# Conv accumulators, z gate, SSD outputs and the scaled x in PSUM instead of SBUF

## The chip, the core and the metric

One core of one Trainium2 chip. The metric is the device time of one execution in microseconds (us); the median of three runs of the kernel before is 935.29 us.

## The reference, cut to what matters

One decoder layer, on a prompt of 1024 tokens and on 8 samples of 8 tokens, with a width of 1024, all in float32:

- h = RMSNorm(x); one projection gives z (1024 columns), xBC (1536), dt, pool inputs and gates.
- xBC goes through a causal depthwise convolution of width 4 (four taps per channel plus a bias) and SiLU. It gives x (16 heads of 64), B and C (2 groups of 128 states).
- SSD in chunks of 128 tokens, per head: y = (mask(C Bt) * decay) (x*dt) + exp(acum) * (C h), and the state h is multiplied by the chunk's decay and gets Bt (x*dt*decay_to_end) added.
- y + d_skip * x, times SiLU(z), then a grouped RMSNorm; a pooling branch beside it; two branch maps with sigmoid gates, an output projection, a norm and the residual.

## The kernel before

Activations lie with channels on the 128 partitions and tokens along the free dimension: 1088 columns (1024 prompt tokens, 64 sample tokens) in three chunks of 256, 384 and 448. A product with a weight matrix takes three float32r passes (hi*hi, lo*hi, hi*lo), so one group of a slab of 128 output channels and one chunk is 24 matmuls of 128x256, 128x384 or 128x448 into one PSUM bank.

The order of the work is written out by slots. `main[t]` is one such group of matmuls. `at_pe(t, f)` puts f's TensorE work ahead of it, `at(t, f, key)` puts work of the other engines behind it, sorted by key. Each engine runs its instructions in that order. So in slot t the other engines work on what the slots before have left, while TensorE runs `main[t]`.

The stages that the change touches:

- **Conv** (slots 0 to 36, twelve slabs). Group t gives three steps: `evac` in slot t+1 (ScalarE copies the bank to R in SBUF and writes A = R * tap 0 + bias; GpSimd fills the three halo columns of R), `taps` in slot t+2 (three VectorE operations A = R shifted * tap + A, key 5: the last of the slot), `fin` in slot t+3 (ScalarE tanh, VectorE (T+1)*A into the tile of x, B or C, key 1).
- **SSD units** (`Unit`: chunk c, four heads u). Units of the first state group run one to a slot in slots 22 to 37, beside conv. Those of the second group run two to a slot in slots 40 to 48, beside the z gates. For a unit at slot t: `xT` in slot t-2 (TensorE transposes x into a bank `xb`, for every second unit B and C too), `prep` (VectorE: x0 = x*dt), `xprod` (GpSimd: x1 = x0*decay_to_end), and in slot t-1 `xsplit` (ScalarE copies x1 to hi, VectorE subtracts to lo); in slot t `mats` (TensorE, into a bank `pyo` for y and a bank `pst` for the state), `fade` (GpSimd), `out` (VectorE: two operations on E, two on x) and `state` (VectorE). `bc_post` splits B and masks C Bt out of the same `xb` bank.
- **Z gates** (`ZTile.gate`, slots 38 to 61): ScalarE tanh, VectorE (T+1)*z into T, VectorE x*0.5*T.

Scratch tiles of 512 columns come from `rt`, a pool of six SBUF buffers that rotates. PSUM has eight banks: two each of `m0` (the groups), `pyo`, `xb` and `pst`.

Of the kernel before, what the change touches and what calls it, by code (L numbers as in the profile page):

```python
# [13 lines left out]
ALU = mybir.AluOpType  # L14
# [23 lines left out]
def hybrid_decoder_step(  # L38
# [258 lines left out]
    class Conv:  # L297
# [14 lines left out]
        def group(self, c):  # L312
            t, box = group3(self.slab, c, hrhs)
            at(t + 1, self.evac, c, box, key=0)
            at(t + 2, self.taps, c, key=5)
            at(t + 3, self.fin, c, key=1)
            return t

        def evac(self, c, box):
            a, b = CHUNKS[c]  # L320
            i = self.i
            n = min(b, LP) - a
            w = n if c < 2 else n + 88
            ps = box["ps"]
            if c == 0:
                self.alloc()
            R = self.R[c] = rt(3 + w)
            if c == 0:
                nc.gpsimd.memset(R[:, 0:3], 0.0)
            else:  # L330
                m = CHUNKS[c - 1][1] - CHUNKS[c - 1][0]
                nc.gpsimd.tensor_copy(R[:, 0:3], self.R[c - 1][:, m:m + 3])
            nc.scalar.copy(R[:, 3:3 + n], ps[:, 0:n])  # L333
            if c == 2:
                Rs = R[:, 3 + n:].rearrange("p (b q) -> p b q", q=11)
                nc.gpsimd.tensor_copy(Rs[:, :, 0:3], histc[i // 6][:, i % 6].rearrange("p (b k) -> p b k", b=8))
                nc.scalar.copy(Rs[:, :, 3:11], ps[:, n:n + NS].rearrange("p (b t) -> p b t", b=8))
                nc.gpsimd.tensor_copy(coll[:, i, 0:3], R[:, n:n + 3])
                nc.gpsimd.tensor_copy(coll[:, i, 3:27].rearrange("p (b k) -> p b k", b=8), Rs[:, :, 8:11])
            A = self.A[c] = rt(w)  # L340
            nc.scalar.activation(A, R[:, 0:w], AF.Identity, bias=cb(i), scale=cw(0, i))

        def taps(self, c):
# [24 lines left out]
    class DtStep:  # L368
# [43 lines left out]
                nc.scalar.copy(self.dtr[:, a:b], box[c][:, 0:b - a])  # L412

        def tok(self):
            self.pd = [bank("pst"), bank("pst"), bank("pyo")]
            for t in range(9):
                n = 128 if t < 8 else NS
                nc.tensor.transpose(self.pd[t // 4][0:n, 128 * (t % 4):128 * (t % 4) + 128], self.dtr[:, 128 * t:128 * t + n], ident)
            zfree(self.dtr)
# [57 lines left out]
    class Unit:  # L477
# [6 lines left out]
        def place(self, t):  # L484
# [5 lines left out]
                at_pe(t - 4 - (self.g == 0), self.bcT, 0)  # L490
                at(t - 4, self.bc_post, 0, key=0 if self.g else 3)
            at_pe(t - 2, self.xT, first=self.g == 1)
            at(t - 2, self.xprod, key=1.5)
            at(t - 1, self.xsplit, key=0 if self.g else -8)
            at(t - 2, self.prep, key=-1 if self.g else 0)
            if self.u % 2 == 0 and self.c < 7:
                at(t - 2, self.bc_post, self.c + 1, key=-2.4 if self.g else 0.6)
# [44 lines left out]
        def prep(self):  # L542
            v = lambda t: t.rearrange("p (a h q) -> p a h q", h=4, q=64)
            if self.g and self.c % 3 == 2:
                x0, xx = rt(256), rt(512)
            else:
                x0, xx = stl([128, 256], "sx", 4), stl([128, 512], "sy", 4)
            x0, self.xx = v(x0)[:, 0], v(xx.bitcast(F32R))
            self.x0 = x0
            nc.vector.tensor_tensor(x0, self.px[:, 0:256].rearrange("p (h q) -> p h q", h=4), bc(dtv[:, self.c, self.hd], 64), op=ALU.mult)  # L550

        def xprod(self):
            self.x1 = rt(256).rearrange("p (h q) -> p h q", h=4)
            nc.gpsimd.tensor_tensor(self.x1, self.x0, bc(dte[:, self.c, self.hd], 64), op=ALU.mult)

        def xsplit(self):
            split(self.xx[:, 0], self.xx[:, 1], self.x1)
# [39 lines left out]
        def out(self):  # L597
            py = self.py
            if self.c:
                E = self.E  # L600
                nc.vector.tensor_tensor(E, py[:, 256:512].rearrange("p (i l) -> p i l", i=2), E, op=ALU.mult)
                nc.vector.tensor_tensor(E, py[:, 0:256].rearrange("p (i l) -> p i l", i=2), E, op=ALU.add)  # L602
            for i in range(2):
                j = 2 * self.u + i
                xv = X[j][:, self.cols]
                nc.vector.scalar_tensor_tensor(xv, xv, dsk[:, j:j + 1], self.E[:, i] if self.c else py[:, 128 * i:128 * i + 128],  # L606
                                               op0=ALU.mult, op1=ALU.add)

        def endT(self):
# [169 lines left out]
    class ZTile:  # L779
# [8 lines left out]
        def gate(self, c, box):  # L788
# [659 lines left out]
    for n in range(2, len(sl)):  # L1448
# [42 lines left out]
```

## Time and profile before

| | |
|---|---|
| median of three runs | 935.29 us (934.77 to 936.5) |
| span of the profiled execution, first to last instruction | 933.1 us |
| TensorE busy in it | 898.7 us (96%) |
| VectorE busy | 574.2 us (62%) |
| ScalarE busy | 349.3 us |
| GpSimd busy | 276.8 us |
| mean granted TensorE clock | 0.988 |

The page gives the span, 933.1 us; what lies around the span in a run is the 2.2 us up to the median. Engine names in the rows: PE = TensorE matmul, DVE = VectorE, ACT = ScalarE, POOL = GpSimd, SP = SyncE. The tiles of an instruction are written out<-in, with buffer numbers left out. Conv and SSD fill the stretch from 44 to 309 us; from 399 us on TensorE is busy without a break until 820 us.

### The profile page before, as it was taken

How to read it: one execution, taken by the hardware profiler on the slowest of the kernel's cores; microseconds unless marked ns; L12 is line 12 of the kernel's file. 1: busy time of each engine (PE TensorE's matmuls, PEld its weight loads, DVE VectorE, ACT ScalarE, POOL GpSimd, SP SyncE). 2: the span in 40 equal slices, each digit the busy share in tenths (PEclk: the TensorE clock that was granted, in tenths of full speed). 3: DMA queues.
4: the chain of work that ended last, by engine and by line, in shares of the span. 5: the costliest groups of instructions: out<-in, count | busy, mean ns of one | idle time of the engine just before them, and what ended most of it. 6: DMA issues, size and time to landing. Idle time of an engine off the chain costs nothing.

```text
span 933.1 us, 14345 instructions
## 1 busy us (share of the span) xinstructions
PE 898.7 (96%) x5568; PEld 828.5 (89%) x5568; DVE 574.2 (62%) x1012; ACT 349.3 (37%) x763; POOL 276.8 (30%) x335
## 2 busy tenths in 40 slices
PE   7979999998989999999999999999999999999997
PEld 5968889897878987899999999999999999988886
DVE  6898799999999788775722333355523231493322
ACT  6525566674862445341311111333232112351211
POOL 6372267675775444311300000000000000370101
PEclk9999999999999999999999999999999999999999
DMA  7010324323422453312121112111121121433232
GB/s 264 8 45 24 97 68 132 79 64 113 134 87 64 124 159 91 91 34 57 46 57 35 37 48 66 53 52 31 49 59 36 35 57 34 145 93 112 68 112 92
DMA packets 101933, 71.24 MB, mean 76 GB/s; under 512 B 7526, under 2 KB 91210, under 8 KB 101865
## 3 DMA queue, kind: packets, MB, share of 16 engines
q1 hardware_dynamic: 101721, 70.19, 25.8%
q8 instruction: 44, 0.72, 0.3%
q14 instruction: 24, 0.20, 0.1%
q10 hardware_dynamic: 144, 0.13, 0.0%
HBM read 60.55 MB, written 9.76 MB: 75 GB/s over the span
## 4 chain that ended last, share of the span: by engine, by line
PE 70%; DVE 17%; ACT 4%; issue 3%; POOL 1%; DMA 1%; SPq 0%; POOLq 0%; ACTq 0%; DVEq 0%
PE m L142 31%; PE pyo L142 23%; DVE r L347 6%; PE m L1380 3%; PE pyo L1380 3%; PE xb L1380 2%; PE pst L1380 2%; DVE z L355 2%; DVE z L606 2%; PE pyo L579 1%; DVE sy L94 1%; DVE z L376 1%; PE pyo L576 1%; DMA z<-dss 1%; DVE se L602 1%
## 5 line engine op out<-in xcount | busy, mean ns | idle before, releaser
L142 PE MATMUL m<-Hhi,whi 128*128 128x384 f32 (+2 forms) x736 | 247.7, 337 | 4.9 <-ACT r L333 4.5
L142 PE MATMUL m<-Hlo,whi 128*128 128x384 f32 (+2 forms) x736 | 243.6, 331 | 0.0
L142 PE MATMUL m<-Hhi,wlo 128*128 128x384 f32 (+2 forms) x736 | 243.5, 331 | 0.0
L94 DVE TENSOR_TENSOR wlo<-raw,whi 128x512 fp32r<-128x512 f32 (+1 forms) x47 | 46.5, 990 | 177.7 <-ACT whi L93 177.6
L142 PEld LDWEIGHTS m<-Hhi,whi 128*128 128x128 f32 x736 | 140.8, 191 | 10.5 <-ACT r L333 4.9
L142 PEld LDWEIGHTS m<-Hlo,whi 128*128 128x128 f32 x736 | 140.6, 191 | 3.4
L142 PEld LDWEIGHTS m<-Hhi,wlo 128*128 128x128 f32 x736 | 140.3, 191 | 3.6
L142 PE MATMUL pyo<-Hhi,whi 128*128 128x256 f32 (+2 forms) x320 | 104.6, 327 | 0.0
L142 PE MATMUL pyo<-Hhi,wlo 128*128 128x256 f32 (+2 forms) x320 | 104.5, 327 | 0.0
L142 PE MATMUL pyo<-Hlo,whi 128*128 128x256 f32 (+2 forms) x320 | 104.4, 326 | 0.0
L347 DVE SCALAR_TENSOR_TENSOR r<-r,par,r 128x256 f32<-128x256 f32 (+2 forms) x108 | 95.3, 883 | 2.5
L93 ACT CAST whi<-raw 128x1024 fp32r<-128x1024 f32 (+1 forms) x67 | 59.6, 889 | 72.0 <-PE m L142 53.9
L94 POOL TENSOR_TENSOR wolo<-r,wohi 128x512 fp32r<-128x512 f32 x16 | 25.1, 1605 | 137.6 <-ACT wohi L93 137.6
L142 PE MATMUL m<-z,whi 128*128 128x448 f32 (+2 forms) x252 | 63.3, 331 | 2.1 <-DVE q L1119 2.1
L142 PEld LDWEIGHTS pyo<-Hlo,whi 128*128 128x128 f32 x320 | 60.6, 189 | 2.4
L142 PEld LDWEIGHTS pyo<-Hhi,whi 128*128 128x128 f32 x320 | 60.5, 189 | 2.4
L142 PEld LDWEIGHTS pyo<-Hhi,wlo 128*128 128x128 f32 x320 | 60.6, 189 | 2.3
L94 POOL TENSOR_TENSOR wlo<-raw,whi 128x1024 fp32r<-128x1024 f32 x20 | 50.9, 2546 | 33.1 <-ACT whi L93 31.2
L142 PEld LDWEIGHTS m<-z,whi 128*128 128x128 f32 x252 | 45.3, 192 | 4.2 <-DVE q L1119 2.3
L142 PE MATMUL m<-z,wlo 128*128 128x256 f32 (+2 forms) x140 | 46.3, 331 | 0.0
L142 PE MATMUL pyo<-z,whi 128*128 128x384 f32 (+2 forms) x180 | 46.1, 332 | 0.0
L568 POOL TENSOR_TENSOR sa<-sa,cb 128x512 f32<-128x512 f32 x28 | 38.2, 1367 | 1.6 <-ACT sa L564 1.6
(388 smaller groups left out, 1656.4 us busy)
## 6 DMA issues: line engine op xcount, KB each, us to landing
raw<-in_w_in_dram SPq DMA_DIRECT2D x43, 512.0 KB, 3.8
sa<-dscr SPq DMA_DIRECT2D x28, 256.0 KB, 4.4
z<-in_x_prompt_dram SPq DMA_DIRECT2D x8, 512.0 KB, 6.0
raw<-in_w_branch_a_dram SPq DMA_DIRECT2D x16, 256.0 KB, 2.6
r<-in_w_out_dram SPq DMA_DIRECT2D x16, 256.0 KB, 3.9
q<-in_x_prompt_dram SPq DMA_DIRECT2D x8, 512.0 KB, 3.6
se<-dscr SPq DMA_DIRECT2D x56, 64.0 KB, 3.5
out_dram<-q SPq DMA_DIRECT2D x14, 256.0 KB, 2.1
```

Of the source, the lines that this page charges most:

```text
L93: nc.scalar.copy(hi, src)
L94: (eng or nc.vector).tensor_tensor(lo, src, hi.bitcast(F32), op=ALU.subtract)
L142: nc.tensor.matmul(ps[:, 0:b - a], slab.w(k, p), rhs(k, p)[:, a:b], start=k == 0 and p == 0, stop=k == slab.kn - 1 and p == 2)
L347: nc.vector.scalar_tensor_tensor(A, R[:, k:k + w], cw(k, i), A, op0=ALU.mult, op1=ALU.add)
L355: nc.vector.scalar_tensor_tensor(self.o[:, a:a + n], T[:, 0:n], 1.0, A[:, 0:n], op0=ALU.add, op1=ALU.mult)
L376: (nc.gpsimd if k % 2 else nc.vector).tensor_tensor(self.h[k], Hhi[:, k].bitcast(F32), Hlo[:, k].bitcast(F32), op=ALU.add)
L568: nc.gpsimd.tensor_tensor(A, A, CBs[self.c, self.g].unsqueeze(1).to_broadcast([128, 4, 128]), op=ALU.mult)
L576: nc.tensor.matmul(py[64 * q:64 * q + 64, 128 * i:128 * i + 128], x0[:, 2 * i + q], A[:, 2 * i + q], start=True, stop=True)
L579: nc.tensor.matmul(py[:, 256 + 128 * i:384 + 128 * i], hs[:, 128 * i:128 * i + 128], Ct[self.g][:, self.cols], start=True, stop=True)
L602: nc.vector.tensor_tensor(E, py[:, 0:256].rearrange("p (i l) -> p i l", i=2), E, op=ALU.add)
L606: nc.vector.scalar_tensor_tensor(xv, xv, dsk[:, j:j + 1], self.E[:, i] if self.c else py[:, 128 * i:128 * i + 128], op0=ALU.mult, op1=ALU.add)
L1380: nc.tensor.matmul(box["ps"][:, 0:b - a], lh, rh[k][:, a:b], start=k == 0 and i == 0, stop=k == 7 and rh is Wlo)
```

## The change

Five edits, and two that make room for them:

- A, the conv accumulator, lies in a PSUM bank `cva` (two buffers) for every group from slot 4 on but the last one. `fin` gets key -0.5, ahead of `evac` in its slot, because a new A takes the bank of the one that `fin` lets go.
- `xprod` goes: x1 = x0*decay_to_end is now a VectorE operation in `prep`, in place in the `xb` bank, and `xsplit` reads it there, in slot t-2 instead of t-1.
- `out` adds into the `pyo` bank instead of E, and the two operations on x read that bank.
- `ZTile.gate` writes (T+1)*z into the bank of the group instead of T.
- `deal` gives out the four banks of `xb` and `pst`: from slot 5 to slot 38 there is one `xb`, one `pst` and two `cva`; outside of that two and two as before. `tok` takes an `xb` for its second bank. `common_post(1)` gets key -3, ahead of the unit's use of the single `pst`.

```diff
--- before.py
+++ after.py
@@ -83,7 +83,19 @@
     def ct(shape, name, dt=F32):
         return cst.tile(shape, dt, name=name)
 
+    qx = {}
+
+    def deal(**bufs):
+        if qx:
+            qx["ctx"].__exit__(None, None, None)
+        qx["ctx"] = tc.tile_pool(name=nm("qx"), bufs=1, space=bass.MemoryType.PSUM)
+        qx["pool"], qx["bufs"] = qx["ctx"].__enter__(), bufs
+
+    deal(xb=2, pst=2)
+
     def bank(tag):
+        if tag in qx["bufs"]:
+            return qx["pool"].tile([128, 512], F32, tag=tag, bufs=qx["bufs"][tag], name=nm(tag))
         return px.tile([128, 512], F32, tag=tag, name=nm(tag))
 
     def tiny(shape):
@@ -313,7 +325,7 @@
             t, box = group3(self.slab, c, hrhs)
             at(t + 1, self.evac, c, box, key=0)
             at(t + 2, self.taps, c, key=5)
-            at(t + 3, self.fin, c, key=1)
+            at(t + 3, self.fin, c, key=-0.5)
             return t
 
         def evac(self, c, box):
@@ -337,7 +349,7 @@
                 nc.scalar.copy(Rs[:, :, 3:11], ps[:, n:n + NS].rearrange("p (b t) -> p b t", b=8))
                 nc.gpsimd.tensor_copy(coll[:, i, 0:3], R[:, n:n + 3])
                 nc.gpsimd.tensor_copy(coll[:, i, 3:27].rearrange("p (b k) -> p b k", b=8), Rs[:, :, 8:11])
-            A = self.A[c] = rt(w)
+            A = self.A[c] = bank("cva")[:, 0:w] if "cva" in qx["bufs"] and (self.i, c) != (7, 2) else rt(w)
             nc.scalar.activation(A, R[:, 0:w], AF.Identity, bias=cb(i), scale=cw(0, i))
 
         def taps(self, c):
@@ -412,7 +424,7 @@
                 nc.scalar.copy(self.dtr[:, a:b], box[c][:, 0:b - a])
 
         def tok(self):
-            self.pd = [bank("pst"), bank("pst"), bank("pyo")]
+            self.pd = [bank("pst"), bank("xb"), bank("pyo")]
             for t in range(9):
                 n = 128 if t < 8 else NS
                 nc.tensor.transpose(self.pd[t // 4][0:n, 128 * (t % 4):128 * (t % 4) + 128], self.dtr[:, 128 * t:128 * t + n], ident)
@@ -490,8 +502,7 @@
                 at_pe(t - 4 - (self.g == 0), self.bcT, 0)
                 at(t - 4, self.bc_post, 0, key=0 if self.g else 3)
             at_pe(t - 2, self.xT, first=self.g == 1)
-            at(t - 2, self.xprod, key=1.5)
-            at(t - 1, self.xsplit, key=0 if self.g else -8)
+            at(t - 2, self.xsplit, key=-0.9 if self.g else 0.1)
             at(t - 2, self.prep, key=-1 if self.g else 0)
             if self.u % 2 == 0 and self.c < 7:
                 at(t - 2, self.bc_post, self.c + 1, key=-2.4 if self.g else 0.6)
@@ -547,11 +558,9 @@
                 x0, xx = stl([128, 256], "sx", 4), stl([128, 512], "sy", 4)
             x0, self.xx = v(x0)[:, 0], v(xx.bitcast(F32R))
             self.x0 = x0
-            nc.vector.tensor_tensor(x0, self.px[:, 0:256].rearrange("p (h q) -> p h q", h=4), bc(dtv[:, self.c, self.hd], 64), op=ALU.mult)
-
-        def xprod(self):
-            self.x1 = rt(256).rearrange("p (h q) -> p h q", h=4)
-            nc.gpsimd.tensor_tensor(self.x1, self.x0, bc(dte[:, self.c, self.hd], 64), op=ALU.mult)
+            x = self.x1 = self.px[:, 0:256].rearrange("p (h q) -> p h q", h=4)
+            nc.vector.tensor_tensor(x0, x, bc(dtv[:, self.c, self.hd], 64), op=ALU.mult)
+            nc.vector.tensor_tensor(x, x0, bc(dte[:, self.c, self.hd], 64), op=ALU.mult)
 
         def xsplit(self):
             split(self.xx[:, 0], self.xx[:, 1], self.x1)
@@ -598,12 +607,13 @@
             py = self.py
             if self.c:
                 E = self.E
+                y = py[:, 0:256].rearrange("p (i l) -> p i l", i=2)
                 nc.vector.tensor_tensor(E, py[:, 256:512].rearrange("p (i l) -> p i l", i=2), E, op=ALU.mult)
-                nc.vector.tensor_tensor(E, py[:, 0:256].rearrange("p (i l) -> p i l", i=2), E, op=ALU.add)
+                nc.vector.tensor_tensor(y, y, E, op=ALU.add)
             for i in range(2):
                 j = 2 * self.u + i
                 xv = X[j][:, self.cols]
-                nc.vector.scalar_tensor_tensor(xv, xv, dsk[:, j:j + 1], self.E[:, i] if self.c else py[:, 128 * i:128 * i + 128],
+                nc.vector.scalar_tensor_tensor(xv, xv, dsk[:, j:j + 1], py[:, 128 * i:128 * i + 128],
                                                op0=ALU.mult, op1=ALU.add)
 
         def endT(self):
@@ -791,9 +801,9 @@
             ps = box["ps"]
             T = rt(b - a)
             nc.scalar.activation(T, ps[:, 0:b - a], AF.Tanh, scale=0.5)
-            nc.vector.scalar_tensor_tensor(T[:, 0:n], T[:, 0:n], 1.0, ps[:, 0:n], op0=ALU.add, op1=ALU.mult)
+            nc.vector.scalar_tensor_tensor(ps[:, 0:n], T[:, 0:n], 1.0, ps[:, 0:n], op0=ALU.add, op1=ALU.mult)
             xv = X[self.j][:, a:a + n]
-            nc.vector.scalar_tensor_tensor(xv, xv, 0.5, T[:, 0:n], op0=ALU.mult, op1=ALU.mult)
+            nc.vector.scalar_tensor_tensor(xv, xv, 0.5, ps[:, 0:n], op0=ALU.mult, op1=ALU.mult)
             if c == 2:
                 nc.vector.scalar_tensor_tensor(zs[:, self.j], T[:, n:n + NS], 1.0, ps[:, n:n + NS], op0=ALU.add, op1=ALU.mult)
 
@@ -1190,7 +1200,7 @@
     at_pe(20, common_pe, 0, first=True)
     at(20, common_post, 0, key=6)
     at_pe(p2 + 10, common_pe, 1, first=True)
-    at(p2 + 10, common_post, 1, key=6)
+    at(p2 + 10, common_post, 1, key=-3)
     
     def reuse(g):
         zfree(Bt[g], Ct[g])
@@ -1202,6 +1212,8 @@
     at(p2 + 19, pad_c, 0, key=8)
     at(p2 + 19, reuse, 0, key=9)
     p3 = len(main)
+    post[5].insert(0, (-99, -1, lambda: deal(xb=1, pst=1, cva=2), ()))
+    at(p3 + 1, lambda: deal(xb=2, pst=2), key=90)
     at(p3 + 4, pad_c, 1, key=8)
     zts = [ZTile(j) for j in range(8)]
     for j in range(4):
@@ -1452,6 +1464,8 @@
         if n + 1 < len(sl):
             at(t_conv, sl[n + 1][1].dma, key=4)
 
+    ctx.callback(lambda: qx["ctx"].__exit__(None, None, None))
+
     for t in range(len(main) + 2):
         for fn, args in pe[t]:
             fn(*args)
```

What VectorE has in one slot of the first state group, from the last taps of one conv group to the next, before (names: r and cva are conv accumulators, z the tiles of x, B and C, sx is x0, sy the split x1, se is E, hst the state, m and cb the split B and the masked product):

```order
L347 SCALAR_TENSOR_TENSOR r_1761<-r_1758,par,r_1761 128x256 x3
L94 TENSOR_TENSOR sy_1843<-r_1855,sy_1843 128x256
L550 TENSOR_TENSOR sx_1923<-xb_1876,dtv 128x256
L601 TENSOR_TENSOR se_1833<-pyo_1865,se_1833 128x256
L602 TENSOR_TENSOR se_1833<-pyo_1865,se_1833 128x256
L606 SCALAR_TENSOR_TENSOR z_347<-z_347,dsk,se_1833 128x128
L606 SCALAR_TENSOR_TENSOR z_388<-z_388,dsk,se_1833 128x128
L595 TENSOR_TENSOR hst<-hst,pst_1872 128x256
L94 TENSOR_TENSOR m_1931<-xb_1876,m_1931 128x128
L518 TENSOR_TENSOR cb_1934<-xb_1876,tri 128x128
L355 SCALAR_TENSOR_TENSOR z_1757<-r_1936,r_1761 128x256
L347 SCALAR_TENSOR_TENSOR r_1840<-r_1837,par,r_1840 128x384 x3
```

And the same slot of the changed kernel:

```order
L359 SCALAR_TENSOR_TENSOR cva_1765<-r_1762,par,cva_1765 128x256 x3
L367 SCALAR_TENSOR_TENSOR z_1761<-r_1913,cva_1765 128x256
L562 TENSOR_TENSOR sx_1925<-xb_1877,dtv 128x256
L563 TENSOR_TENSOR xb_1877<-sx_1925,dte 128x256
L106 TENSOR_TENSOR sy_1926<-xb_1877,sy_1926 128x256
L611 TENSOR_TENSOR se_1833<-pyo_1866,se_1833 128x256
L612 TENSOR_TENSOR pyo_1866<-pyo_1866,se_1833 128x256
L616 SCALAR_TENSOR_TENSOR z_350<-z_350,dsk,pyo_1866 128x128
L616 SCALAR_TENSOR_TENSOR z_391<-z_391,dsk,pyo_1866 128x128
L604 TENSOR_TENSOR hst<-hst,pst_1873 128x256
L106 TENSOR_TENSOR m_1936<-xb_1877,m_1936 128x128
L529 TENSOR_TENSOR cb_1939<-xb_1877,tri 128x128
```

The last operation of conv (L355, now L367) has moved from the end of the slot to right behind the taps that it depends on, x1 (L563) has come from GpSimd, and its split (L106) stands right behind it instead of a slot later.

ScalarE in the same slot, before (r_1936 is the tanh of this slot, r_1914 the next R, r_1921 the next accumulator, sa the decay of a unit, whi a weight slab):

```order
L93 CAST sy_1843<-r_1855 128x256
L333 COPY r_1914<-m_298_1804 128x384
L337 COPY r_1914<-m_298_1804 128x8x8
L341 ACTIVATE r_1921<-r_1914,par 128x472
L93 CAST m_1931<-xb_1876 128x128
L354 ACTIVATE r_1936<-r_1761 128x256
L93 CAST whi_1942<-raw_1698 128x1024
L563 ACTIVATE sa_1831<-sa_1831,acm 128x128 x4
L564 ACTIVATE sa_1831<-sa_1831 128x512
```

And in the changed kernel:

```order
L366 ACTIVATE r_1913<-cva_1765 128x256
L345 COPY r_1916<-m_293_1806 128x384
L349 COPY r_1916<-m_293_1806 128x8x8
L353 ACTIVATE cva_1923<-r_1916,par 128x472
L105 CAST sy_1926<-xb_1877 128x256
L105 CAST m_1936<-xb_1877 128x128
L105 CAST whi_1942<-raw_1701 128x1024
L572 ACTIVATE sa_1831<-sa_1831,acm 128x128 x4
L573 ACTIVATE sa_1831<-sa_1831 128x512
```

The tanh (L354, now L366) has moved ahead of the copy that frees a bank of the groups, and the cast of x1 behind the writing of the next accumulator.

## Rows read from the trace of the kernel before

**Rows 1.** Windows by stage: length, busy us of PE, PEld, DVE, ACT, POOL, clock, DMA, GB/s.
```profile
44.00:129.00 85.00, 76.76 (x481) 69.59 (x481) 72.49 (x100) 41.87 (x88) 40.16 (x49) 0.98 0.22 61
129.00:214.20 85.20, 82.53 (x591) 74.93 (x591) 83.30 (x164) 57.05 (x144) 62.51 (x76) 1.00 0.29 80
214.20:241.20 27.00, 24.31 (x148) 21.81 (x146) 25.76 (x51) 15.28 (x41) 15.08 (x20) 0.94 0.33 99
241.20:309.50 68.30, 65.08 (x474) 58.21 (x474) 61.61 (x136) 33.74 (x90) 42.48 (x46) 0.98 0.36 104
309.50:398.90 89.40, 86.56 (x633) 77.12 (x632) 74.91 (x135) 40.44 (x83) 40.10 (x26) 0.98 0.41 115
398.90:820.00 421.10, 421.10 (x2548) 406.13 (x2548) 175.06 (x317) 109.96 (x214) 31.61 (x45) 1.00 0.19 53
```

**Rows 2.** Waits of PE, whole span: us in total, times, longest us.
```profile
PE m L142 <- ACT r L333: 4.5, 1, 4.5
PE pyo L579 <- DVE hst L595: 2.8, 1, 2.8
PE xb L538 <- DVE sx L550: 2.7, 1, 2.7
```

**Rows 3.** Timeline from 52.58: start, us, engine, line, operation, tiles, shapes, count.
```profile
52.58 2.89 POOL L376 TENSOR_TENSOR z<-Hhi,Hlo 128x1088 f32<-128x1088 f32 x1
52.99 6.98 DVE L376 TENSOR_TENSOR z<-Hhi,Hlo 128x1088 f32<-128x1088 f32 x2
...
55.42 3.40 POOL L94 TENSOR_TENSOR wlo<-raw,whi 128x1024 fp32r<-128x1024 f32 x1
```

**Rows 4.** Groups of DVE, 129 to 214.2: count, busy us, mean ns, idle before.
```profile
L347 DVE SCALAR_TENSOR_TENSOR r<-r,par,r 128x256 f32<-128x256 f32 (+2 forms) x42 | 39.9, 951 | 1.0
L606 DVE SCALAR_TENSOR_TENSOR z<-z,dsk,se 128x128 f32<-128x128 f32 x22 | 9.1, 456 | 0.4
L94 DVE TENSOR_TENSOR sy<-r,sy 128x256 fp32r<-128x256 f32 x14 | 8.5, 609 | 0.0
...
L606 DVE SCALAR_TENSOR_TENSOR z<-z,dsk,pyo 128x128 f32<-128x128 f32 x4 | 1.2, 336 | 0.0
```

**Rows 5.** Timeline of DVE alone, from 200.74 on.
```profile
200.74 0.41 DVE L94 TENSOR_TENSOR sy<-r,sy 128x256 fp32r<-128x256 f32 x1
201.08 0.41 DVE L550 TENSOR_TENSOR sx<-xb,dtv 128x256 f32<-128x256 f32 x1
201.41 0.41 DVE L601 TENSOR_TENSOR se<-pyo,se 128x256 f32<-128x256 f32 x1
201.85 0.42 DVE L602 TENSOR_TENSOR se<-pyo,se 128x256 f32<-128x256 f32 x1
...
203.18 0.55 DVE L355 SCALAR_TENSOR_TENSOR z<-r,r 128x384 f32<-128x384 f32 x1
```

**Rows 6.** Chain of work in order of time, from 75.67: start us, us, what.
```profile
75.67 0.63 DVE r L347
...
80.93 0.72 DVE r L347
81.65 0.02 issue
81.67 0.61 ACT r L354
```

**Rows 7.** Groups of ACT, 129 to 214.2.
```profile
L354 ACT ACTIVATE r<-r 128x472 f32<-128x472 f32 (+2 forms) x15 | 7.6, 505 | 0.7 <-DVE sy L94 0.7
...
L93 ACT CAST sy<-r 128x256 fp32r<-128x256 f32 x14 | 5.6, 401 | 6.8 <-POOL r L554 6.8
```

**Rows 8.** Groups of DVE, 241.2 to 309.5.
```profile
L606 DVE SCALAR_TENSOR_TENSOR z<-z,dsk,se 128x128 f32<-128x128 f32 x28 | 17.5, 664 | 0.5
L796 DVE SCALAR_TENSOR_TENSOR z<-z,r 128x384 f32<-128x384 f32 (+1 forms) x10 | 7.9, 795 | 0.3
...
L794 DVE SCALAR_TENSOR_TENSOR r<-r,m 128x384 f32<-128x384 f32 (+1 forms) x9 | 4.5, 497 | 0.0
```

## The prediction, made before the changed kernel was run

> **What bounds the kernel now.** I read the windows by stage first. From 398.9 to 820 us TensorE is busy for all of its 421.1 us, and the change touches nothing there. What can be won lies in the five windows from 44 to 398.9 us, where TensorE is idle for 8.2, 2.7, 2.7, 3.2 and 2.8 us, 19.6 us in all [rows 1]. In the second of them, slots 22 to 35 with one SSD unit and one conv group each, a slot takes 85.2/14 = 6.09 us; TensorE works 5.90 us of it and VectorE 5.95: both are all but full. Its idle 1.9 us are the gaps between operations that depend on each other: 201.41 + 0.41 to 201.85 is 0.03, where one that doesn't depend starts 0.08 before the end of the last (201.08 to 201.41 for an operation of 0.41) [rows 5]. So VectorE never truly waits there, and sets the pace together with TensorE.
>
> Next the waits of TensorE: the long ones are for VectorE, or for a ScalarE copy that waited for it [rows 2].
>
> Then the reason why VectorE is slow. At 52.99 it begins two sums of two SBUF tiles while GpSimd is in one of its own; they take 6.98 us, and GpSimd's next operation is stretched to 3.40 [rows 3]. The two engines take turns wherever VectorE reads two SBUF tiles. The same shape shows the price: the operation on x takes 456 ns with E in SBUF and 336 with the second input in PSUM; a conv tap takes 951 ns on average [rows 4], but 0.63 (384 columns) or 0.72 (472) when nothing is in its way [rows 6]; by the slope 256 columns take 0.50, so the mean of the three is 0.61.
>
> **The change, part by part, in slots 22 to 35.** All per slot, on VectorE.
>
> Taken away: 42 taps x (0.95 - 0.61) = 14.3 us; 22 operations on x x (0.456 - 0.336) = 2.6; 14 splits of x1, whose hi and lo now meet one SBUF input, x (0.609 - 0.41) = 2.8 [rows 4, 5]. Together 19.7 us, 1.41 us a slot.
>
> Added: x1, 128x256, costs 0.41 like the other operations of this shape [rows 5]. As it needs the one before it, 0.08 of overlap and 0.03 of a gap come on top: 0.52. It still reads two SBUF tiles (x0 and the decay), so GpSimd may still hold it up: between 0 and the 0.20 that the split suffers now [rows 4, 5]. I take 0.1, since GpSimd loses one of its four long operations of the slot.
>
> Added as a wait: the split of x1 stands right behind x1, and ScalarE's cast of 0.40 lies between [rows 7], with 0.02 for each hand-over [rows 6]: 0.44. Before, GpSimd and a slot of distance hid it. Behind the waiting split are `out`, `state` and the taps, and TensorE's next unit waits for the first two.
>
> Added as a second wait: `fin` now follows its own taps. Taps, tanh of 0.505 [rows 7], two hand-overs of 0.02 [rows 6], and the 0.08 of overlap that the last tap had: 0.63. Before, six or more operations lay between.
>
> The new slot is 6.09 - 1.41 + 0.52 + 0.1 + 0.44 + 0.63 = 6.37; for a full slot, one in which `out` has its two operations on E (0.44 each, twelve of 14 units), 6.5. I take 6.45, which is 0.36 over the old one: 14 x 0.36 = +5.0 us. Against that VectorE starts with a lead: slots 20 and 21 have no `out` and `state` yet (from 201.41 to 203.18 is 1.77 us each [rows 5]), and the units of slots 22 and 23 have no operations on E, 0.9 each: 5.3 us. So the stage ends about where it did: **0 us**. Ends: -2.5 (TensorE's idle time goes) and +6.
>
> Single `xb` and `pst`: TensorE's transposes of slot s+1 wait for split, `bc_post` and `state` of slot s. In a slot of VectorE these are done three taps, some 1.9 us, before its end, and the transposes take less than the taps, so the next `prep` finds them ready. I cost this at nothing as long as VectorE sets the pace; what it costs when it doesn't is within the +6.
>
> What an operation costs that writes into PSUM the trace does not show: VectorE has none. Reading: 336 against the 456 of SBUF, and L602, PSUM and SBUF, takes 0.42 like L94's 0.41 from SBUF alone. For writing I bound it by 0 below and by the loss of the overlap, 0.08 each, above: three taps, x1 and one addition, 0.40 a slot, 5.6 us in the stage. I take 0, the value that reading shows.
> The Trainium skill speaks against that (VectorE: DVE Perf Modes, section "The TRN2 errata"): it gives a VectorE operation a fixed part of 58 cycles from SBUF and 120 from PSUM. By it, as an estimate from that page, each operation moved to PSUM would lose 65 ns, some eight a slot, about half a microsecond, and the stage would end some 7 us later. The 336 ns with PSUM beside the 456 ns without [rows 4] disagree for reading, so I don't follow it in the sum.
>
> **The other stages.** Slots 36 to 39 (214 to 241 us): the 2.7 us for `xb` are VectorE's backlog, paid when two units a slot begin [rows 2]. With single banks TensorE can't run ahead of VectorE, so there is less to pay, and the second pair of banks is back by then: **-2.0** (ends 0 and -2.7).
>
> Slots 40 to 48: VectorE loses 28 x (0.664 - 0.336) = 9.2, 10 gates x (0.795 - 0.497) = 3.0 and some 15 x 0.2 = 3.0 on splits, 15.2 us [rows 8, 4]; it gets 16 x 0.45 = 7.2 for x1 (two `prep` stand together, so the first cast is hidden) and some 0.15 a slot for the second cast: 8.5. It gains 6.7 us in a stage where TensorE is idle for 3.2 [rows 1], waiting for the state (2.8) [rows 2]: **-2.5** (ends 0 and -3.2).
>
> Slots 49 to 61: the gates lose their lock, but few of TensorE's 2.8 idle us hang on them: **-0.5** (ends +1 and -2.8).
>
> Slots 5 to 21: 8.2 us idle. The longest, 4.5, was a copy out of the bank of a group that waited for a scratch tile of `rt`; A no longer takes one, so that wait goes. But that copy now stands behind the tanh, and that behind the taps of the slot before, which stand behind VectorE's two sums of Hhi and Hlo (6.98 with GpSimd's turns [rows 3]). The copy moves from one wait to another: **-1.0** (ends -6 and +3).
>
> Sum: 0 - 2.0 - 2.5 - 0.5 - 1.0 = -6.0. The profiled execution's span is 933.1, so 927.1; what lies around the span is the 2.2 us up to the median of 935.3. Forecast **929.3 us**.
>
> **Rivals.**
> 1. *TensorE becomes the only bound.* If the two waits for ScalarE cost less than I say and the sums no longer block the copies, two thirds of the 19.6 idle us go: -13, 922 us. For it: VectorE has little else to wait for. Against it: the new waits lie on VectorE's own path, in every slot.
> 2. *Slower: VectorE's slot gets longer than its old one by more than its lead.* Place: slots 22 to 37. If x1 meets GpSimd as the split does now (+0.1) and writing to PSUM costs the overlap (+0.4), the slot is 6.95 and the stage ends 14 x 0.86 - 5.3 = 6.7 later; the same two prices, twice a slot, eat the 2.5 us of slots 40 to 48, and the copies behind the tanh lose 1.0 instead of winning it: +6.7 - 2.0 - 0.5 + 1.0 = +5.2, 940.5 us. It decides from a slot of some 6.9 us on, where 14 x 0.8 - 5.3 = 5.9 uses up the gain of all other stages. For it: both waits are certain, and single banks leave no room. Against: the lock that goes is worth 1.4 us a slot. The rule of the Trainium skill cited above (VectorE: DVE Perf Modes, section "The TRN2 errata") would end in this rival too, by its dearer PSUM operands; of the rival's chance I give it 0.06.
> 3. *No change.* The lock goes and the waits come, and TensorE's own work, 5.90 of the 6.09, hides the rest in every stage: 935 us.
> That the change doesn't do what it says can't be: the rows of the order show the operands in PSUM; only x1 keeps two SBUF inputs.
>
> **How the numbers follow.** Forecast 0.46, rival 1 0.14, rival 2 0.27, rival 3 0.13. A measurement of this kernel tells 0.2%, 1.9 us, from no change. Faster: 0.14 and most of the forecast's 0.46, whose own range is 925 to 934: 0.56. Same: rival 3 and the forecast's upper edge: 0.15. Slower: rival 2 and a little: 0.29. The range goes from rival 1 to just past rival 2, without their outer tails: 922 to 941.
>
> **What would show it.** Right: taps near 0.61 us on average and operations on x near 0.34; a gap of about 0.44 on VectorE before each split and of about 0.55 before each `fin`, released by ScalarE; a slot of 6.3 to 6.6 between 129 and 214 us; idle TensorE of less than 1 us from 241 to 309. Wrong: taps that still take 0.9 us, so that the lock was not their reason; a stage from 129 to 214 that is over 5 us longer; or an x1 of 0.6 us and more. My forecast fails if the first two stages change by more than 5 us together.

## The result: slower by half a per cent

The changed kernel takes 940.59 us (median of 4 runs, 939.73 to 941.02), the kernel before 935.89 beside it (4 runs). The ratio is 1.0054, 95% interval 1.004 to 1.0068: slower by 4.7 us, where 6 us faster was forecast. The profiled span is 939.2 us, 6.1 more than before's 933.1.

### The profile page after: what moved, and what is told of

It is laid out like the page before. It is cut to its first block, busy times and chain, and to the rows that moved or that the text cites. A ratio compares the mean times of both kernels' runs of the same rounds, so it can differ in the third digit from the quotient of the medians.

```text
span 939.2 us, 14347 instructions
## 1 busy us (share of the span) xinstructions
PE 897.8 (96%) x5568; PEld 825.1 (88%) x5568; DVE 539.9 (57%) x1044; ACT 349.4 (37%) x763; POOL 238.2 (25%) x303
## 4 chain that ended last, share of the span: by engine, by line
PE 73%; DVE 15%; ACT 4%; issue 4%; POOL 3%; DMA 1%; SPq 0%; POOLq 0%; ACTq 0%; DVEq 0%
PE m L154 34%; PE pyo L154 22%; DVE cva L359 3%; PE m L1392 3%; PE pyo L1392 3%; PE xb L1392 2%; PE pst L1392 2%; DVE xb L563 2%; DVE z L616 1%; ACT r L366 1%; DVE z L367 1%; PE pyo L588 1%; PE pyo L585 1%; DMA z<-dss 1%; POOL z L388 1%
## 5 line engine op out<-in xcount | busy, mean ns | idle before, releaser
L106 DVE TENSOR_TENSOR wlo<-raw,whi 128x512 fp32r<-128x512 f32 (+1 forms) x47 | 46.6, 991 | 177.6 <-ACT whi L105 177.6
L106 POOL TENSOR_TENSOR wolo<-r,wohi 128x512 fp32r<-128x512 f32 x16 | 25.1, 1606 | 137.6 <-ACT wohi L105 137.6
L106 POOL TENSOR_TENSOR wlo<-raw,whi 128x1024 fp32r<-128x1024 f32 x20 | 47.8, 2389 | 46.7 <-ACT whi L105 35.8
L359 DVE SCALAR_TENSOR_TENSOR cva<-r,par,cva 128x472 f32<-128x472 f32 (+2 forms) x93 | 56.7, 610 | 2.2
L577 POOL TENSOR_TENSOR sa<-sa,cb 128x512 f32<-128x512 f32 x28 | 36.4, 1301 | 9.3 <-ACT sa L573 9.3
```

The lines of the kernel that those rows point to most:

```text
L106: (eng or nc.vector).tensor_tensor(lo, src, hi.bitcast(F32), op=ALU.subtract)
L359: nc.vector.scalar_tensor_tensor(A, R[:, k:k + w], cw(k, i), A, op0=ALU.mult, op1=ALU.add)
L577: nc.gpsimd.tensor_tensor(A, A, CBs[self.c, self.g].unsqueeze(1).to_broadcast([128, 4, 128]), op=ALU.mult)
```

## The profile after

The windows of the changed kernel, cut at the starts of the same slots as [rows 1] (length, then busy us of PE, PEld, DVE, ACT, POOL, granted clock, DMA share, GB/s):

```profile
42.50:128.20 85.70, 77.45 (x484) 70.06 (x482) 60.63 (x109) 43.88 (x97) 38.54 (x50) 0.98 0.22 60
128.20:223.60 95.40, 85.58 (x591) 76.91 (x590) 78.47 (x180) 55.60 (x136) 42.07 (x61) 0.98 0.30 83
223.60:249.40 25.80, 22.96 (x149) 20.45 (x147) 22.18 (x48) 14.56 (x39) 8.09 (x12) 1.00 0.19 61
249.40:316.30 66.90, 63.59 (x472) 56.80 (x473) 53.20 (x146) 33.83 (x91) 33.15 (x33) 1.00 0.37 109
316.30:405.10 88.80, 86.59 (x634) 77.16 (x633) 69.09 (x135) 40.27 (x83) 39.30 (x26) 0.98 0.40 114
405.10:826.00 420.90, 420.90 (x2547) 405.95 (x2546) 175.10 (x317) 109.86 (x214) 31.91 (x45) 1.00 0.19 53
```

One window loses much: slots 22 to 35, 95.4 us for 85.2. The first loses 0.7, the later ones with slots of the change win 1.2, 1.4 and 0.6 us. In the losing window VectorE is busy for *less* than before (78.5 for 83.3), and still the stage is longer. So I look at what VectorE does and waits for there, its groups in that window against [rows 4] (count, busy us and mean ns of one, then the idle time before and what ended it):

```profile
L359 DVE SCALAR_TENSOR_TENSOR cva<-r,par,cva 128x384 f32<-128x384 f32 (+2 forms) x41 | 25.1, 612 | 1.0
L563 DVE TENSOR_TENSOR xb<-sx,dte 128x256 f32<-128x256 f32 x14 | 12.4, 888 | 0.5
L616 DVE SCALAR_TENSOR_TENSOR z<-z,dsk,pyo 128x128 f32<-128x128 f32 x28 | 8.5, 345 | 0.4
L367 DVE SCALAR_TENSOR_TENSOR z<-r,cva 128x384 f32<-128x384 f32 (+1 forms) x14 | 7.1, 507 | 7.4 <-ACT r L366 7.4
L106 DVE TENSOR_TENSOR sy<-xb,sy 128x256 fp32r<-128x256 f32 x14 | 5.9, 425 | 6.9 <-ACT sy L105 6.9
L562 DVE TENSOR_TENSOR sx<-xb,dtv 128x256 f32<-128x256 f32 x14 | 5.9, 418 | 0.7 <-PE xb L549 0.5 <-PE xb L522 0.2
L612 DVE TENSOR_TENSOR pyo<-pyo,se 128x256 f32<-128x256 f32 x12 | 5.2, 432 | 0.4
```

What was to get cheaper did: taps 612 ns, operations on x 345, splits 425. The idle column is new: 7.4 us behind the tanh and 6.9 behind the cast, one wait of each kind in every slot. Before, the split waited for nothing [rows 4], and the last operation of conv for 0.6 us in all:

```profile
L355 DVE SCALAR_TENSOR_TENSOR z<-r,r 128x384 f32<-128x384 f32 (+1 forms) x14 | 7.1, 504 | 0.6 <-ACT r L354 0.6
```

And x1 (L563) takes 888 ns, twice an operation of its shape. Busy and waiting together are 78.5 + 14.3 = 92.8 of the 95.4 us.

One slot shows all three. VectorE from the x1 of slot 28 on, in order of time:

```profile
168.81 1.48 DVE L563 TENSOR_TENSOR xb<-sx,dte 128x256 f32<-128x256 f32 x1
170.78 0.42 DVE L106 TENSOR_TENSOR sy<-xb,sy 128x256 fp32r<-128x256 f32 x1 [0.49 <-ACT sy L105]
...
173.29 1.93 DVE L359 SCALAR_TENSOR_TENSOR cva<-r,par,cva 128x384 f32<-128x384 f32 x3
175.13 0.21 DVE L660 TENSOR_TENSOR m<-pst,btri 64x64 f32<-64x64 f32 x1
175.78 0.55 DVE L367 SCALAR_TENSOR_TENSOR z<-r,cva 128x384 f32<-128x384 f32 x1 [0.44 <-ACT r L366]
```

and of the same kernel's timeline, the x1 of slot 27, which has no GpSimd operation beside it, and the one GpSimd operation beside the x1 of slot 28:

```profile
162.99 0.43 DVE L563 TENSOR_TENSOR xb<-sx,dte 128x256 f32<-128x256 f32 x1
...
168.70 1.30 POOL L577 TENSOR_TENSOR sa<-sa,cb 128x512 f32<-128x512 f32 x1
```

The mask on GpSimd (L577) began 0.11 us ahead of the x1 of slot 28 and ran until 170.00; that x1, with its two SBUF inputs, ended at 170.29. A mask runs beside x1 in 7 of the 14 slots, for 7.4 us together. Those seven took 0.78 to 1.51 us each; the other seven, the same operation with the same inputs, 0.43. TensorE's waits over the whole span, as in [rows 2], show who is late:

```profile
PE pst L592 <- DVE hst L604: 6.2, 6, 2.3
PE xb L549 <- DVE cb L529: 3.7, 1, 3.7
PE pst L652 <- DVE hst L604: 2.7, 1, 2.7
PE xb L549 <- DVE sy L106: 2.7, 2, 1.7
```

The first three are waits for a single bank that VectorE has yet to read; the two of the last row lie ahead of the groups of slots 40 and 41, where there are two `xb` again. But a bank can be short, or its reader late. The experiments tell the two apart: theory W says that VectorE is late, by its new waits and x1; theory S, that the single banks are too few.

## The experiments

Each was timed four to six times, beside the kernel before. The table is worked out from the traces: stage lengths between the starts of TensorE's conv or z groups, and for slots 22 to 35 the busy time of the engines and VectorE's waits for ScalarE (the tanh and the casts, added up), in us.

| | before | changed | E1 | E2 | E3 | E4 | E5 | E6 | E7 | E8 | E9 |
|---|---|---|---|---|---|---|---|---|---|---|---|
| time (median) | 935.9 | 940.6 | 928.5 | 927.1 | 917.9 | 940.4 | 962.3 | 931.5 | 930.2 | 920.5 | 921.9 |
| slots 5 to 21 | 85.0 | 85.6 | 85.4 | 82.8 | 81.8 | 86.8 | 84.8 | 86.6 | 85.1 | 83.7 | 83.1 |
| slots 22 to 35 | 85.2 | 95.5 | 84.2 | 83.7 | 82.6 | 90.3 | 102.3 | 87.6 | 85.4 | 83.3 | 83.6 |
| slots 36 to 39 | 27.0 | 25.7 | 26.9 | 25.2 | 22.2 | 24.6 | 32.5 | 24.7 | 25.8 | 22.2 | 23.7 |
| slots 40 to 48 | 68.3 | 67.0 | 64.2 | 68.5 | 64.2 | 69.5 | 75.0 | 65.7 | 67.0 | 64.2 | 65.6 |
| 22 to 35: TensorE busy | 82.5 | 85.6 | 82.2 | 82.1 | 81.9 | 85.1 | 88.3 | 83.7 | 83.0 | 81.9 | 82.1 |
| 22 to 35: VectorE busy | 83.3 | 78.5 | 81.7 | 75.3 | 68.7 | 83.0 | 92.8 | 70.7 | 74.5 | 67.1 | 71.3 |
| its waits for ScalarE | 0.6 | 14.3 | 1.2 | 1.4 | 4.0 | 0 | 7.3 | 14.8 | 7.1 | 2.3 | 1.3 |

**E1: out and gates alone, on the kernel before.**

```diff
+                y = py[:, 0:256].rearrange("p (i l) -> p i l", i=2)
...
-                nc.vector.tensor_tensor(E, py[:, 0:256].rearrange("p (i l) -> p i l", i=2), E, op=ALU.add)
+                nc.vector.tensor_tensor(y, y, E, op=ALU.add)
...
-            nc.vector.scalar_tensor_tensor(T[:, 0:n], T[:, 0:n], 1.0, ps[:, 0:n], op0=ALU.add, op1=ALU.mult)
+            nc.vector.scalar_tensor_tensor(ps[:, 0:n], T[:, 0:n], 1.0, ps[:, 0:n], op0=ALU.add, op1=ALU.mult)
```

> The kernel before, with two parts of the change alone: out adds in pyo's bank, and the z gate's product stays in the bank of its group. Conv accumulators, x1, its place in the order and the double banks stay as before. If the loss comes from the new waits of VectorE on ScalarE and from x1 (theory W), or from the single banks (theory S), nothing of either is here, so only the gain is left: operations on x at 0.34 us instead of 0.46 (slots 22 to 35) and 0.66 (slots 40 to 48), gates at 0.5 instead of 0.8. Both theories: slots 22 to 35 shorter by 1 to 3 us (22 x 0.12 = 2.6 on VectorE), slots 36 to 48 shorter by 2 to 3; 930 to 933 us, ratio 0.994 to 0.998. If writing sums into PSUM were what costs (a third theory), the addition in pyo would take over 0.5 us and nothing would be won: 935 and more.

Measured: 928.47 us, ratio 0.993 (0.9916 to 0.9944). Faster, and more than expected: slots 22 to 35 win 0.9 us, a little less than expected, slots 40 to 48 win 4.1, more. The third theory falls. VectorE's groups of this kernel in slots 40 to 48, beside [rows 8]:

```profile
L607 DVE SCALAR_TENSOR_TENSOR z<-z,dsk,pyo 128x128 f32<-128x128 f32 x32 | 9.7, 344 | 0.5
L94 DVE TENSOR_TENSOR sy<-r,sy 128x256 fp32r<-128x256 f32 x11 | 9.1, 849 | 0.0
L603 DVE TENSOR_TENSOR pyo<-pyo,se 128x256 f32<-128x256 f32 x14 | 6.1, 432 | 0.5
L602 DVE TENSOR_TENSOR se<-pyo,se 128x256 f32<-128x256 f32 x14 | 5.8, 417 | 2.5 <-PE pyo L579 2.4
...
L797 DVE SCALAR_TENSOR_TENSOR z<-z,m 128x384 f32<-128x384 f32 (+1 forms) x9 | 4.6, 509 | 0.3
```

L603 writes into PSUM and L602 into SBUF, with the same inputs: 432 and 417 ns. The splits (L94), which the edit doesn't touch, rise from 593 to 849 ns: they now lie beside GpSimd's operations for 8.5 us instead of 4.6. A part of the gain moves to another operation as a loss.

**E2: the changed kernel, x0 and x1 ahead of fin, the split behind it.**

```diff
-            at(t - 2, self.xsplit, key=-0.9 if self.g else 0.1)
-            at(t - 2, self.prep, key=-1 if self.g else 0)
+            at(t - 2, self.xsplit, key=-0.9 if self.g else -0.45)
+            at(t - 2, self.prep, key=-1 if self.g else -0.8)
```

> The changed kernel with one more move in slots 7 to 35: x0 and x1 are computed ahead of fin, and the split of x1 behind fin, so that the tanh runs beside x0 and x1 and the cast beside fin. Theory W (VectorE's two waits on ScalarE, 0.5 and 0.5 us a slot, lengthen the slot): both waits fall under 0.15 us, VectorE's slot is 0.9 us shorter, the stretch of slots 22 to 35 goes from 95.4 back to 83 to 88 us, 930 us and less. Theory S (TensorE waits for the single xb and pst banks in each slot, whatever VectorE's order): the waits of VectorE go too, but the stretch stays at 92 us or more and the time at 937 or more, with PE's waits for pst and xb as long as they are (15 us in all).

Measured: 927.10 us, ratio 0.9911 (0.9889 to 0.9932). Two numbers of order, no instruction and no bank more, take 13.5 us off the changed kernel, 11.7 of them in slots 22 to 35. VectorE's waits in those slots, longest sums first:

```profile
DVE sx L562 <- PE xb L549: 3.2, 4, 0.9
DVE sx L562 <- PE xb L522: 1.9, 2, 1.1
DVE sy L106 <- ACT sy L105: 1.2, 6, 0.3
```

Now VectorE waits for TensorE. TensorE's waits there are down to two:

```profile
PE pst L592 <- DVE m L660: 0.8, 1, 0.8
PE pst L652 <- DVE hst L604: 0.8, 1, 0.8
```

In the changed kernel TensorE's waits for `pst` in these slots are 9.8 us. Theory W holds and theory S falls: with the same single banks, 1.6 us of waits are left once their reader is on time. x1 is shorter here too, 673 ns on average; E6 and E9 separate that from the waits.

**E3: the changed kernel, x1 on GpSimd again.**

```diff
-            nc.vector.tensor_tensor(x, x0, bc(dte[:, self.c, self.hd], 64), op=ALU.mult)
...
+        def xprod(self):
+            self.x1 = rt(256).rearrange("p (h q) -> p h q", h=4)
+            nc.gpsimd.tensor_tensor(self.x1, self.x0, bc(dte[:, self.c, self.hd], 64), op=ALU.mult)
...
-            at(t - 2, self.xsplit, key=-0.9 if self.g else 0.1)
+            at(t - 2, self.xprod, key=1.5)
+            at(t - 1, self.xsplit, key=0 if self.g else -8)
```

> The changed kernel with x1 made by GpSimd again, in SBUF, and its split a slot later, as before the change. Conv accumulators and sums stay in PSUM, xb and pst stay single. Theory W: VectorE loses x1 (0.89 us with its contention) and the wait for the cast (0.49) in each slot and gets back some 0.2 on the split; its slot goes from 6.8 to about 5.8, so TensorE sets the pace again: slots 22 to 35 in 83 to 87 us, 929 to 932 us in all. Theory S: the wait for pst stays, since state still follows in the same order, and the stretch is 90 us and more, 935 us or more.

Measured: 917.92 us, ratio 0.9814 (0.9797 to 0.9832), the best version found: 2.4% below the changed kernel, 1.9% below the one before. Theory W's sign, but 11 us more than it said: against the changed kernel slots 5 to 21 win 3.8, slots 36 to 39 win 3.5 and slots 40 to 48 win 2.7, which I had not counted. Slots 22 to 35 and 40 to 48 of this kernel, in the columns of the first fence:

```profile
124.37:207.00 82.63, 81.93 (x593) 74.68 (x591) 68.71 (x169) 56.45 (x142) 50.16 (x74) 1.00 0.34 94
229.22:293.44 64.22, 63.26 (x475) 56.76 (x474) 52.58 (x133) 31.92 (x85) 40.20 (x45) 1.00 0.39 113
```

TensorE is idle for 0.7 and 1.0 us. All the rest of the change is in this kernel, the single banks included.

**E4: single banks alone, on the kernel before** (with the order of `common_post` and the bank of `tok` that go with them).

```diff
+    post[5].insert(0, (-99, -1, lambda: deal(xb=1, pst=1), ()))
+    at(p3 + 1, lambda: deal(xb=2, pst=2), key=90)
...
-    at(p2 + 10, common_post, 1, key=6)
+    at(p2 + 10, common_post, 1, key=-3)
```

> The kernel before with single xb and pst banks alone, in the stretch in which the change has them; conv accumulators, x1, out and gates as before. Theory W: VectorE's slot is unchanged (6.1 us), TensorE's transposes find their banks free: slots 22 to 35 no more than 1 us longer, 935 to 937 us. Theory S: TensorE waits in slots with little other work, some 0.2 to 0.4 us a slot, 3 to 6 us in slots 22 to 35 and several us more in slots 5 to 21, 939 to 943 us.

Measured: 940.41 us, ratio 1.0052 (1.0037 to 1.0068), as theory S said, though not in the way it said. TensorE's waits in slots 22 to 35:

```profile
PE pst L595 <- DVE m L662: 3.6, 1, 3.6
PE pst L595 <- DVE hst L607: 0.8, 1, 0.8
PE pst L595 <- DVE hst L605: 0.6, 1, 0.6
```

It is not a little in each slot: one wait of 3.6 us at the common step of group 1, where `common_pe` takes the only `pst` and VectorE is behind. Of the 5.2 us that this window loses, 4.0 lie in slots 28 to 30. In the kernel before VectorE is just as full as TensorE, so a single bank has a price there. The loss of E4 is as large as that of the whole change, but it isn't the same loss: E2, E3 and E9 have the same single banks, wait 0.7 to 1.6 us for `pst` in this window and are faster than the kernel before.

**E5: x1's move alone, on the kernel before, two banks each.**

```diff
-            nc.vector.tensor_tensor(x0, self.px[:, 0:256].rearrange("p (h q) -> p h q", h=4), bc(dtv[:, self.c, self.hd], 64), op=ALU.mult)
-
-        def xprod(self):
...
+            x = self.x1 = self.px[:, 0:256].rearrange("p (h q) -> p h q", h=4)
+            nc.vector.tensor_tensor(x0, x, bc(dtv[:, self.c, self.hd], 64), op=ALU.mult)
+            nc.vector.tensor_tensor(x, x0, bc(dte[:, self.c, self.hd], 64), op=ALU.mult)
```

> The kernel before with one part of the change alone: x1 on VectorE into the xb bank, its split right behind it. Two banks each for xb and pst, conv accumulators, fin, out and gates as before. Theory X (x1 on VectorE and the wait of its split for ScalarE's cast cost a slot, and no second bank can win that back): VectorE gets 0.7 to 0.9 for x1 and 0.5 for the wait, and gives back 0.2 on the split, so its slot goes from 6.1 to some 7.2 us; the stretch of slots 22 to 35 gets 8 to 13 us longer, 943 to 950 us. Theory S (x1 and the wait cost little as long as two banks let TensorE run ahead): at most 3 us longer, 935 to 938 us.

Measured: 962.33 us, ratio 1.0283 (1.0269 to 1.0296). Theory X, and above its range: slots 22 to 35 lose 17.1 us, the slots behind them another 12. Two banks each did not prevent it. VectorE's groups in slots 22 to 35:

```profile
L603 DVE SCALAR_TENSOR_TENSOR z<-z,dsk,se 128x128 f32<-128x128 f32 x22 | 13.6, 660 | 0.4
L551 DVE TENSOR_TENSOR xb<-sx,dte 128x256 f32<-128x256 f32 x14 | 11.2, 802 | 0.5
...
L94 DVE TENSOR_TENSOR sy<-xb,sy 128x256 fp32r<-128x256 f32 x14 | 5.9, 425 | 7.3 <-ACT sy L93 7.3
```

x1 and the cast's wait are much as in the changed kernel. What I missed: the operations on x, still with two SBUF inputs here, rise from 456 to 660 ns: five of them now lie beside GpSimd's long weight splits (7.6 us of overlap). And TensorE waits for `pst` with two banks too, most of it at and behind the common step of slot 28:

```profile
PE pst L580 <- DVE hst L592: 5.4, 2, 4.2
...
PE pst L639 <- DVE hst L592: 1.8, 1, 1.8
```

**E6: x1 from PSUM alone.** The product of both decays is made once, ahead of the loop.

```diff
+            nc.vector.tensor_tensor(dte[:, 0:8], dte[:, 0:8], dtv[:, 0:8], op=ALU.mult)
...
-            nc.vector.tensor_tensor(x, x0, bc(dte[:, self.c, self.hd], 64), op=ALU.mult)
+            nc.vector.tensor_tensor(x, x, bc(dte[:, self.c, self.hd], 64), op=ALU.mult)
```

> The changed kernel, but x1 is the raw x in its PSUM bank times the product of the two decays, which is computed once ahead of the loop; so x1 reads one SBUF input and no longer needs x0. Order, waits and banks as in the changed kernel. If x1's 0.89 us is the turn that GpSimd's mask has on the SBUF port (theory lock), x1 falls to 0.42 to 0.45, VectorE's slot from 6.8 to 6.35, slots 22 to 35 from 95.4 to 88 to 90 us and the time to 931 to 935. If it is the dependence on x0 and on the bank that x1 is written to (rival), x1 stays at 0.6 and more and the time at 938 or more.

Measured: 931.48 us, ratio 0.9954 (0.994 to 0.9968). The group of x1 in slots 22 to 35:

```profile
L564 DVE TENSOR_TENSOR xb<-xb,dte 128x256 f32<-128x256 f32 x14 | 5.9, 423 | 0.0
```

888 ns became 423, at the same place in the order, with a mask beside it in 6 of the 14 slots and both waits about as long as in the changed kernel (7.0 and 7.8 us). x1 needs neither x0 nor a second SBUF tile now, but it still writes the bank, so that half of the rival is out; the other half, the dependence on x0, falls by the seven x1 of the changed kernel without a mask beside them, which depend on x0 too and took 0.43 us. A mask that runs beside x1 no longer stretches it, which is what the lock theory says. The stretch got 7.9 us shorter.

**E7: x0, x1 and the split ahead of fin; only the tanh is hidden.**

```diff
-            at(t - 2, self.xsplit, key=-0.9 if self.g else 0.1)
-            at(t - 2, self.prep, key=-1 if self.g else 0)
+            at(t - 2, self.xsplit, key=-0.9 if self.g else -0.7)
+            at(t - 2, self.prep, key=-1 if self.g else -0.8)
```

> The changed kernel with x0, x1 and the split of x1 moved ahead of fin: the tanh now runs beside x0 and x1, while the wait of the split for the cast stays. With both waits hidden slots 22 to 35 took 83.7 us, as against 95.4 in the changed kernel. If each wait costs by its length (0.5 us a slot each), this kernel stands about half way: 88 to 91 us in the stretch, 931 to 935 us in all. If the slot is lost only where VectorE gets over TensorE's pace of 5.9 us, removing one of two waits gets nearly all of it back: 84 to 86 us, 927 to 930 us.

Measured: 930.24 us, ratio 0.9947 (0.9935 to 0.996). The stretch takes 85.4 us, near the second reading, by which losses end where VectorE gets down to TensorE's pace. But two things changed at once. VectorE's group of x1 here:

```profile
L563 DVE TENSOR_TENSOR xb<-sx,dte 128x256 f32<-128x256 f32 x14 | 8.5, 604 | 0.5
```

x1 stands less beside the mask and wins 0.28 us itself, so the tanh's part of the gain isn't measured alone.

**E8: E3 with x0 ahead of fin.**

```diff
-            at(t - 2, self.prep, key=-1 if self.g else 0)
+            at(t - 2, self.prep, key=-1 if self.g else -0.8)
```

> The best of the two repairs together: the changed kernel with x1 on GpSimd and its split a slot later, and x0 ahead of fin, so that the tanh has work beside it. With x1 on GpSimd alone TensorE was idle for 0.7 us of the 82.6 of slots 22 to 35, and VectorE waited for TensorE there. If TensorE sets the pace (theory), nothing more can be won: 82 to 83 us in the stretch and 917 to 919 us in all. If VectorE's last waits for the tanh (1.2 us) still count (rival), 1 us less in the stretch and 2 or more in slots 7 to 21: 914 to 916 us.

Measured: 920.45 us, ratio 0.9838 (0.9825 to 0.985). Not better than E3. The stretch is 83.3 us, so the theory's main point stands, but slots 5 to 21 took 83.7 us instead of 81.8. Of these 1.9 us 1.6 lie in slot 21, where TensorE's granted clock was 0.57 from 119.5 to 123.5 us; in E3's slot 21 it was 1.00. Why it fell here is open.

**E9: both repairs that leave x1 on VectorE** (the edits of E6 and E2 together).

> The changed kernel with both repairs that leave x1 on VectorE: x1 read from PSUM alone (0.42 us instead of 0.89), and x0 and x1 ahead of fin with the split behind it, so that tanh and cast have work beside them. If the stretch of slots 22 to 35 takes the longer of TensorE's 82 to 83 us and of VectorE's work with its waits plus some 2 us (theory pace), VectorE has 70.7 of work and about 1.3 of waits here, so TensorE sets the pace: 82.5 to 84 us in the stretch, and 920 to 925 us in all, faster than either repair alone (927 and 931). If x1 on VectorE costs by itself, through the bank of xb that it holds longer (rival bank), TensorE waits for xb in many slots: 86 us and more in the stretch, 927 and more in all.

Measured: 921.88 us, ratio 0.986 (0.9837 to 0.9884), the stretch 83.6 us: theory pace. Its group of x1:

```profile
L564 DVE TENSOR_TENSOR xb<-xb,dte 128x256 f32<-128x256 f32 x14 | 5.9, 422 | 0.0
```

x1 is as long as in E6, so E6 and E9 differ by the waits alone: 14.8 us of them there, 1.3 here, and 3.9 us of the stretch, which ends 1.5 us above TensorE's own work. From 95.5 us in the changed kernel, x1's contention takes off 7.9 (E6) and the waits, after it, 3.9. x1 on VectorE isn't bad in itself; its turn with GpSimd and the two uncovered waits are.

## Why the prediction was wrong

**The views and the relief were read rightly.** VectorE paces slots 22 to 35, and the 951 ns of a tap were GpSimd's turns: 612 measured for 0.61, x 345 for 336, split 425 for 0.41.

**PSUM as output costs next to nothing**, as I took it: 432 beside 417 ns in E1. Nor does reading from it: 417 ns for L602 of E1 and 425 for a split from PSUM, beside 0.41 us for a split from SBUF alone [rows 5]. The Trainium skill (VectorE: DVE Perf Modes, section "The TRN2 errata") would make an operation that reads from PSUM dearer by 65 ns, as an estimate from its cycles. These 65 ns are not in the runs, and that share of rival 2 falls.

**The two waits were sized well**: 0.44 forecast for the cast's, 0.49 measured (6.9/14); for the tanh's 0.53 of idle time (7.4/14) beside the 0.55 named as its mark. They were certain, and E2 shows them, together with a shorter x1 (673 ns), to be worth 11.7 us of the stretch; by themselves, with x1 out of the way, 3.9 (E6 to E9).

**First failed term: "I take 0.1" for x1's contention.** It is 0.888 - 0.42 = 0.47 us. I had bounded it by what the split suffered (0.20), but that bound belongs to the split's place in the order. x1 came to stand beside the mask in half of the slots, and there it took up to 1.51 us for 0.43: the bound from above was the mask's 1.3 us, not 0.20. The Trainium skill (SBUF — State Buffer, section "SBUF: two separate sides") says of the port pair that VectorE and GpSimd share that the one that starts first gets it "for the whole instruction; the other fully blocks". The trace agrees in the main: the x1 of slot 28, which began 0.11 us after the mask, ended 0.29 us after it and took 1.05 us more than an x1 alone. The slot came to 95.45/14 = 6.82 us for the 6.45 forecast: 14 x 0.37 = +5.2. The prediction had named an x1 of 0.6 us and more, and a stage over 5 us longer, as signs of being wrong; both came.

**Second failed term: the lead of 5.3 us.** Slots 22 to 24 took 17.7 us and slots 25 to 35, without the 2.7 at the common step, 75.1, 6.82 each. Three slots at that pace would be 20.5, so the lead was 2.8: +2.5. Why the rest of it was lost, no run shows.

**Third failed term: single `xb` and `pst` "at nothing as long as VectorE sets the pace".** TensorE waited 2.7 us for the single `pst` at the common step, so I add 2.7. That single banks are not free there E4 shows, where they alone cost 5.2 us of the stretch, 3.6 of it one wait at this step; where VectorE is ahead of TensorE (E2, E3), they cost next to nothing. But E5, with two banks each and VectorE late, waits 1.8 us at the same step and 4.2 behind it. So how much of the 2.7 is the bank's, and how much its late reader's, isn't shown.

5.2 + 2.5 + 2.7 = 10.4; the stage lost 10.3 where 0 was forecast. This fits partly by its making: the lead is reckoned with the 6.82 that slots 25 to 35 give once the 2.7 are taken out. Only the first term has a run of its own on the changed kernel: E6 gives back 7.9 us, 14 x 0.465 = 6.5 of it x1 itself; with it the wait at the common step shrinks to 1.6 us and the granted clock stays at 1.00 in the stretch.

**The other stages.** Slots 36 to 39 won 1.2 (forecast 2.0), slots 40 to 48 1.4 (2.5), slots 49 to 61 0.6 (0.5). Slots 5 to 21 lost 0.6 (forecast -1.0): 3.6 us were won ahead of slot 20, where the copy's wait for a scratch tile is gone, and 3.9 lost in slot 20, where the transposes waited 3.7 for the single `xb`. Rival 2 named the place and, by luck, the time (940.5): 0.4 of the 0.5 us that it added to a slot was PSUM writing, which measured 15 ns for the addition, and 0.1 was x1, which came 0.37 dearer than forecast.

**What the stage follows.** In the table the stretch is the longer of TensorE's 82 to 83 us and of VectorE's busy time with its waits for ScalarE, plus 0.7 to 2.6 us: 83.9 gives 85.2 (before), 92.8 gives 95.5 (changed), 100.1 gives 102.3 (E5), 85.5 gives 87.6 (E6), while 72.7 gives 82.6 (E3). E4 alone stands outside, by its one wait for a bank. How much of E3's gain is the conv in PSUM by itself wasn't tried.

## What to carry to other kernels

Where an operation with two SBUF inputs is moved, price it by the GpSimd operation it will stand beside in its new place, not by what it or its like suffered in the old one; better, give it a PSUM input (E6). A helper's hand-over that becomes back-to-back on an engine costs up to its full length in each slot, as far as that engine sets the pace (of E6's 14.8 us of waits 3.9 came back in E9, then TensorE's work was the limit), and an order that puts other work between needs no instruction more (E2). A part that loses can hide what the others win: E3 is the change with x1 left on GpSimd, at 0.9814 of the time before.

## What was not expected of the hardware

TensorE's idle time can cost it twice (a mean granted clock of 1.00 is the upper level, 2.4 GHz, all the time; under it, a part of the stretch ran at 1.2 GHz). The matmuls of slots 22 to 35 took 81.9 us at a granted clock of 1.00 (E3, 0.7 us idle), 85.6 at 0.98 (changed, 9.8 idle), 85.1 at 0.96 (E4, 5.2 idle) and 88.3 at 0.93 (E5, 14.0 idle). Not all of that is the clock: E6, with 3.9 us idle, took 83.7 at 1.00. Here are E5's stretch and, of the changed kernel's, the part in which the clock was low, right behind the waits at the common step:

```profile
128.81:231.12 102.31, 88.27 (x590) 79.69 (x590) 92.77 (x175) 58.83 (x144) 51.57 (x64) 0.93 0.24 66
175.30:178.70 3.40, 3.31 (x12) 3.31 (x13) 2.39 (x4) 1.28 (x3) 3.13 (x4) 0.52 0.75 223
```

Of the changed kernel's 10.3 us in this stage, 3.1 are longer busy time and 7.2 idle time. Of the 3.1, some 1.6 are the low clock (an estimate: 3.31 us of work at 0.52 instead of 1.00); the rest came at the full clock and is not explained. A longer wait alone doesn't tell whether the clock falls: in slot 20 E9 waited 2.8 us for `xb` and kept 1.00 in the slot behind it, E8 waited 2.0 and fell to 0.50.
